# First mixer: convolution sums in PSUM, unscaled turning of the scores with a late division, bias tables loaded, the scan's small matrices spread

## The chip, the cores and the metric

The kernel runs on one core of one Trainium2 chip. The metric is device time in microseconds. Engines by the names of the profile: PE (matmul; PEld loads its stationary operand), DVE (VectorE), ACT (ScalarE), POOL (GpSimd), SP (which issues most DMAs). [...]

## The reference, cut to what matters

A two-layer encoder over 512 tokens of width 1024. Layer 0 has the mixer of this case:

```python
def conformer_conv(a_val, a_gate, conv_w, conv_b, ln_g, ln_b):
    h = a_val * sigmoid(a_gate)
    h = depthwise_conv(h, conv_w, width 31, centred) + conv_b   # 512 channels
    return silu(layernorm(h, ln_g, ln_b))

def even_mixer(h, w_in, ...):
    a_val, a_gate, q, k, v = split(h @ w_in)
    conv_out = conformer_conv(a_val, a_gate, ...)
    # 8 heads of 64; q, k rms-normed per head
    # three dilated windows, each softmax(q k^T / 8 - slope_h * dist), joined by
    # the softmax of their log-sum-exps
    return concat(conv_out, att) @ w_out
```

The three windows are one softmax over all 512 keys with the bias `log(count of windows that hold the pair) - slope_h * dist`, and that is how the kernel computes them. After the mixer comes a routed mixture of 16 experts, in layer 1 an S5 scan (whose discretised matrices are computed from the parameters `lam_re, lam_im, log_dt`) and a second mixture.

## The kernel before, in words

The program is written in the order in which each engine is to run it: no scheduler moves instructions, each engine takes its own in program order, and semaphores stand where data pass between engines. `mixer0` (L310) has these stretches:

- **Input, 0 to 32 us.** Norm and transposition of x, split into a high and a low part (`xT`), so that a product of three fp32r matmuls per 128 rows (`mm3`, L276) replaces one fp32 matmul. Weights come in blocks of 128 by 2048 (1 MB) over the SP queue into a ring of two buffers; `next_split` (L259) turns a block into `whi` (ACT, L273) and `wlo` (L274, on POOL, or on DVE with `fast`). A block's ring buffer is given back, and the next load issued, once it is split. The split blocks lie alternately in the pools `ipa` and `ipb`, one buffer each.
- **Value and gate, 32 to 66 us.** Four chunks of 128 channels, each a pair of products of 24 matmuls; then sigmoid (ACT) and the product with the value (`hp`, L405, DVE), which frees the two `mm` banks. Chunk by chunk the convolution is queued as a generator of 31 DVE instructions (`conv`, L332: one `tensor_scalar`, L334, then 30 `scalar_tensor_tensor`, L337, which add to `cv` in SBUF). `fill.run(ns)` (L49) issues such instructions until their nominal lengths (400, 663) fill `ns`; the list `FL` says how many go where.
- **q, k, v, to 169 us.** Six blocks (n = 0 to 5) of four tiles of 24 matmuls, 128 by 256. `head_norm` of a tile (square on ACT, L554 sum on DVE, root, L559, L562) comes one tile late, with fill around it; `head_turn` (eight transposes, L192) after the second tile of the next block.
- **Attention, 169 to 273 us.** Seventeen steps; step n handles a pair of heads j = n // 4 and a quarter t of the queries: `recip(n)` (1/sum, and two diagonal matrices `dg`, L465), `scores(n+1)`, `soft(n+1)` (add bias and take the maximum, L451; exp with its sum, L456), `values(n-1)`, `turn(n)`: matmuls with `dg` that transpose the exponentials and divide them at once (L474), copied to SBUF by ACT. `bias` (L429) builds a 128x896 table per head on DVE (L432) from `dist` and `logc`. Three convolution instructions are filled in per step; from step `L0` = 6 one step of the convolution's layer norm follows each; silu at step 14, `ln_out` at 15. At `W0` = 11 and 12 half a block of `w_out` is split, on DVE. `s5_small` (L1003) computes the scan's small matrices in 281 instructions, nearly all on POOL and 128x64; it is started once the q, k, v stretch has been issued and yields twice, before the copies of its table `L` to `PV` and `PC` by ACT and DVE (at steps 7 and 8).
- **Output product, 273 to 335 us.** `w_out` in four blocks, 16 products, with the router's work between; the ring of expert weights opens at its start (`rings`, L632).

Of the kernel before, what the change touches and what calls it, by code (L numbers as in the profile page):

```python
# [20 lines left out]
NT = 4  # L21
# [17 lines left out]
S5N = 7  # L39
L0 = 6  # L40
W0 = 11
WM = 36, 55, 14, 5
FL = 8500, 600, 700, 1700, 1000, 1900


class Fill:
# [13 lines left out]
    def drain(self):  # L60
        self.run(1 << 40)

# [44 lines left out]
class Kern:  # L107
# [202 lines left out]
    def mixer0(self, prep, front):  # L310
# [4 lines left out]
        with ExitStack() as c:  # L315
# [16 lines left out]
            def conv(ch):  # L332
                acc = cv[:, ch]
                v.tensor_scalar(acc, hp[:, ch, 0:S], cw[:, ch, 0:1], cb[:, ch:ch + 1], op0=OP.mult, op1=OP.add)  # L334
                yield 400
                for j in range(1, CW):
                    v.scalar_tensor_tensor(acc, hp[:, ch, j:j + S], cw[:, ch, j:j + 1], acc, op0=OP.mult, op1=OP.add)  # L337
                    yield 663

            with ExitStack() as c2:  # L340
# [69 lines left out]
                self.late_consts()  # L410
                if prep:
                    self.s5_params(mp)

# [3 lines left out]
                dist = mp2.tile([128, 896], F32, name="dist")  # L417
                nc.scalar.dma_start(dist, a["dist"])
                logc = mp2.tile([128, 896], F32, name="logc")
                nc.scalar.dma_start(logc, a["logc"])  # L420
# [22 lines left out]
                def soft(n):  # L443
                    j, t = n // 4, n % 4
                    z = un[n]
                    z["sc"], z["dg"] = [], []
                    u = 384 - 128 * t
                    st = mp2.tile([128, 2, 4], F32, name="ast", bufs=4)
# [8 lines left out]
                    z["st"] = st  # L457

                def recip(n):
                    z = un[n]  # L460
                    st = z["st"]
                    v.reciprocal(st[:, :, 3], st[:, :, 2])
                    for i in range(2):
# [110 lines left out]
                for n in range(6):  # L574
# [3 lines left out]
                    for t in range(NT):  # L578
# [7 lines left out]
                        if n == 5 and t == 0:  # L586
                            bias(0)
# [18 lines left out]
            for n in range(N + 1):  # L606
                if n < N:
                    recip(n)
# [1246 lines left out]
```

## Time and profile before

| | |
|---|---|
| median of 3 runs | 1597.78 us (1596.94 to 1600.73) |
| profiled execution | 1601.47 us, its span 1599.7 us |
| PE busy | 1437.1 us (90%) |
| DVE busy | 760.9 us (48%) |
| ACT busy | 368.7 us (23%) |
| POOL busy | 487.2 us (30%) |
| convolution, L337 | 120 instructions, 121.4 us, mean 1012 ns |
| mixer 0 | about the first 335 us of the span |

How to read it: a busy share is an average over stretches with different limits. "Idle before" of a group is time in which its engine stood still ahead of the group, with the instruction that ended it. [...] L-numbers are lines of the kernel before.

### The profile page before, as it was taken

How to read it: one execution, taken by the hardware profiler on the slowest of the kernel's cores; microseconds unless marked ns; L12 is line 12 of the kernel's file. 1: busy time of each engine (PE TensorE's matmuls, PEld its weight loads, DVE VectorE, ACT ScalarE, POOL GpSimd, SP SyncE). 2: the span in 40 equal slices, each digit the busy share in tenths (PEclk: the TensorE clock that was granted, in tenths of full speed). 3: DMA queues.
4: the chain of work that ended last, by engine and by line, in shares of the span. 5: the costliest groups of instructions: out<-in, count | busy, mean ns of one | idle time of the engine just before them, and what ended most of it. 6: DMA issues, size and time to landing. Idle time of an engine off the chain costs nothing. (4 is left out here: it accounts for less than half of the span.)

```text
span 1599.7 us, 23281 instructions
## 1 busy us (share of the span) xinstructions
PE 1437.1 (90%) x9452; PEld 864.2 (54%) x9452; DVE 760.9 (48%) x1200; ACT 368.7 (23%) x776; POOL 487.2 (30%) x749
## 2 busy tenths in 40 slices
PE   8879888989999999897989775899899999999998
PEld 7778656983443443433344664898533333333335
DVE  4999847350238557575612699423311222221122
ACT  5223446320111111111111521336211111111111
POOL 3425887000025576665510456430100000000000
PEclk9989979989999999999999977999999999999999
DMA  4311004539988999999999985822399999999998
GB/s 160 136 53 54 1 1 158 212 132 360 410 349 340 416 416 412 411 409 416 416 418 419 294 267 177 342 106 106 150 420 419 420 419 419 420 419 420 420 419 330
DMA packets 77708, 482.45 MB, mean 302 GB/s; under 512 B 10017, under 2 KB 12833, under 8 KB 23713
## 3 DMA queue, kind: packets, MB, share of 16 engines
q1 hardware_dynamic: 66032, 455.11, 71.0%
q0 software_dynamic: 5504, 16.19, 2.7%
q10 hardware_dynamic: 6064, 9.66, 1.7%
q8 instruction: 74, 1.21, 0.3%
q14 instruction: 34, 0.27, 0.0%
HBM read 456.88 MB, written 24.05 MB: 301 GB/s over the span
## 5 line engine op out<-in xcount | busy, mean ns | idle before, releaser
L825 PE MATMUL mm<-w,xi 128*64 128x512 f32 x2048 | 472.8, 605 | 39.8 <-DMA w<-in_w_e_up 31.7
L825 PEld LDWEIGHTS mm<-w,xi 128*64 128x64 f32 x2048 | 139.3, 138 | 325.3 <-issue 245.8
L877 PE MATMUL po<-w,h 128*64 128x512 f32 x896 | 205.5, 599 | 0.0
L337 DVE SCALAR_TENSOR_TENSOR cv<-hp,vec,cv 128x512 f32<-128x512 f32 x120 | 121.4, 1012 | 2.9
L877 PEld LDWEIGHTS po<-w,h 128*64 128x64 f32 x896 | 59.0, 136 | 106.2 <-issue 104.5
L767 DVE TENSOR_TENSOR R<-R,ac 128x512 f32<-128x512 f32 x112 | 71.8, 682 | 91.9 <-PE ac L765 91.9
L284 PE MATMUL mm<-whi,xT 128*128 128x256 f32 x512 | 101.4, 297 | 11.9 <-DVE hp L405 10.8
L274 POOL TENSOR_TENSOR wlo<-w,whi 128x1024 fp32r<-128x1024 f32 x26 | 67.1, 2603 | 120.3 <-ACT whi L273 120.3
L850 DVE TENSOR_TENSOR h<-h,mm 128x256 f32<-128x256 f32 x60 | 22.5, 417 | 158.1 <-PE mm L825 158.1
L284 PEld LDWEIGHTS mm<-whi,xT 128*128 128x128 f32 x512 | 85.5, 203 | 14.3 <-DVE hp L405 7.3
L284 PE MATMUL mm<-wlo,xT 128*128 128x256 f32 x256 | 75.2, 294 | 0.0
L849 ACT ACTIVATE h<-mm 128x256 f32<-128x256 f32 x60 | 19.8, 381 | 221.3 <-PE mm L825 221.3
L198 DVE COPY OE<-po 64x512 f32<-64x512 f32 x28 | 19.4, 694 | 105.1 <-ACT OE L196 105.0
L694 DVE TENSOR_TENSOR xi<-tr,vec 128x512 f32<-128x512 f32 x32 | 22.1, 691 | 98.2 <-PE tr L704 57.5
L1578 POOL DMA_DIRECT2D gn<-in_mix_norm_odd x8 | 4.7, 592 | 194.0 <-PE mm L825 156.3
L704 PEld LDWEIGHTS tr<-Dm,hn 128*128 128x128 f32 x512 | 59.4, 196 | 7.3 <-ACT h L849 6.5
L1293 PE MATMUL ac<-w,Hs 128*64 128x128 f32 x256 | 33.9, 402 | 31.7 <-POOL Hs L1280 26.5
L196 ACT ACTIVATE OE<-po 64x512 f32<-64x512 f32 x28 | 16.5, 590 | 194.4 <-PE po L877 194.4
L704 PE MATMUL tr<-Dm,hn 128*128 128x128 f32 x512 | 60.9, 281 | 0.0
L284 PEld LDWEIGHTS mm<-wlo,xT 128*128 128x128 f32 x256 | 52.1, 204 | 0.0
L689 DVE TENSOR_TENSOR Dm<-slot,io 128x512 f32<-128x512 f32 (+1 forms) x16 | 11.4, 711 | 85.2 <-PE tr L192 85.1
L1695 POOL DMA_DIRECT2D Ld<-Lt x32 | 18.4, 581 | 108.6 <-DVE Lt L986 102.4
(395 smaller groups left out, 2550.3 us busy)
## 6 DMA issues: line engine op xcount, KB each, us to landing
w<-in_w_e_gate SPq DMA_DIRECT2D x128, 1024.0 KB, 17.0
w<-in_w_e_up SPq DMA_DIRECT2D x128, 1024.0 KB, 17.1
w<-in_w_e_down SPq DMA_DIRECT2D x112, 1024.0 KB, 16.0
w<-in_w_e_tail SPq DMA_DIRECT2D x16, 1024.0 KB, 19.9
w<-in_w_in SPq DMA_DIRECT2D x9, 1024.0 KB, 4.8
Wd<-Wt ACTq DMA_DIRECT2D x32, 256.0 KB, 10.3
Cd<-CE POOLq DMA_DIRECT2D x16, 512.0 KB, 13.0
w<-Wd SPq DMA_DIRECT2D x8, 1024.0 KB, 14.6
```

Of the source, the lines that this page charges most:

```text
L198: self.nc.vector.tensor_copy(out, in_)
L274: (nc.vector if fast else nc.gpsimd).tensor_tensor(lo[:, o], w[:, o], hi[:, o].bitcast(F32), op=OP.subtract)
L284: self.nc.tensor.matmul(out, st(i, k), mv(j, k), start=n == 0, stop=n == 3 * KC - 1)
L337: v.scalar_tensor_tensor(acc, hp[:, ch, j:j + S], cw[:, ch, j:j + 1], acc, op0=OP.mult, op1=OP.add)
L694: v.tensor_tensor(P[j]["xi"][:, 4 * hf:4 * hf + 4], p.rearrange("p (k c) -> p k c", k=4), g[:, 4 * hf:4 * hf + 4].unsqueeze(2).to_broadcas ...
L704: nc.tensor.matmul(p[:, k * 128:(k + 1) * 128], hn[:, s, kk * 128:(kk + 1) * 128], Dm[:, s].rearrange("p e c -> p (e c)"), start=s == 0, s ...
L767: v.tensor_tensor(rv, rv, p, op=OP.add)
L825: nc.tensor.matmul(p[hf * 64:(hf + 1) * 64], xi[:, k, r:r + CAP], w[:, o:o + 512], start=k == 0, stop=k == KC - 1)
L849: nc.scalar.activation(h[:, o], pg[:, o], AF.Silu)
L850: v.tensor_tensor(h[:, o], h[:, o], pu[:, o], op=OP.mult)
L877: nc.tensor.matmul(po[dh * 64:(dh + 1) * 64], hT[:, c4 * 128 + hf * 64:c4 * 128 + hf * 64 + 64], w[:, o:o + 512], start=i == 0, stop=i == 7)
L1293: nc.tensor.matmul(ov, lh, rh, start=n == 0, stop=n == 2)
```

## The change

1. **Convolution.** `conv` takes a PSUM bank (`self.ac()`) as its accumulator; 29 of the 30 adding instructions read and write it, and the last writes the result to `cv` in SBUF.
2. **Turning.** `turn` transposes the unscaled exponentials (PE transposes against the identity); the copies to SBUF go to ACT for the first head and DVE for the second. `recip` comes after `turn` and makes `dg` on ACT. After the fourth quarter of a head pair, `values` spreads the reciprocals over 64 rows with eight fp32 matmuls (`ones` against `dg`) into an `ac` bank, ACT copies them (`zs`), DVE multiplies (`o`), and only then come the high part (ACT) and the low part (DVE).
3. **Softmax.** The negation of the maximum and the exponential are issued head by head.
4. **Bias.** Eight finished tables come from memory over the SP queue (0.46 MB each): two before q, k, v, four after them, two at step 8. The tables' pool and that of `dg`, `zs`, `o` lie on the right side of SBUF, opened after `iq` and `ipb` are closed.
5. **Scan matrices.** `s5_small` returns a list of 281 single instructions; six are issued per tile of q, k, v (24 tiles), 14 per attention step, so that the list ends at step 9. The temporaries of its exponential get buffers of their own.
6. **Order.** The layer norm starts at step 3 (silu at 11, `ln_out` at 12 and 13); `w_out`'s first block is split at 10 and 11; all splits of `w_out` go to POOL instead of DVE.
7. **Fill.** `FL` goes from 8500, 600, 700, 1700, 1000, 1900 to 9200, 600, 1300, 2000, 1300, 1900. By the nominal lengths that is 14 instead of 13 per chunk, 3 per q and k tile as before, 4 instead of 3 per tile of the first v block, 2 per tile of the second as before.

```diff
-S5N = 7
-L0 = 6
-W0 = 11
+L0 = 3
+W0 = 10
+SM = 6, 14
-FL = 8500, 600, 700, 1700, 1000, 1900
+FL = 9200, 600, 1300, 2000, 1300, 1900
...
             def conv(ch):
-                acc = cv[:, ch]
+                acc = self.ac()
...
-                    v.scalar_tensor_tensor(acc, hp[:, ch, j:j + S], cw[:, ch, j:j + 1], acc, op0=OP.mult, op1=OP.add)
+                    v.scalar_tensor_tensor(cv[:, ch] if j == CW - 1 else acc, hp[:, ch, j:j + S], cw[:, ch, j:j + 1],
+                                           acc, op0=OP.mult, op1=OP.add)
...
-                def bias(j):
-                    for h in (2 * j, 2 * j + 1):
-                        B = Bh[h] = mp2.tile([128, 896], F32, name="B", bufs=2)
-                        v.scalar_tensor_tensor(B, dist, -(2.0 ** (-(h + 1))), logc, op0=OP.mult, op1=OP.add)
+                def bias(h, pool, bufs):
+                    Bh[h] = pool.tile([128, 896], F32, name="B", bufs=bufs)
+                    nc.sync.dma_start(Bh[h], a["bias"][h])
...
+                        v.tensor_scalar(st[:, i, 1:2], st[:, i, 0:1], -1.0, None, op0=OP.mult)
                         z["sc"].append(sc)
-                    v.tensor_scalar(st[:, :, 1], st[:, :, 0], -1.0, None, op0=OP.mult)
-                    for i in range(2):
-                        nc.scalar.activation(z["sc"][i], z["sc"][i], AF.Exp, bias=st[:, i, 1:2], accum_out=st[:, i, 2:3])
+                        nc.scalar.activation(sc, sc, AF.Exp, bias=st[:, i, 1:2], accum_out=st[:, i, 2:3])
...
                         for kc in range(4):
-                            nc.tensor.matmul(p[:, kc * 128:(kc + 1) * 128], z["sc"][i][:, kc * 128:(kc + 1) * 128],
-                                             z["dg"][i], start=True, stop=True)
-                        self.copy(z["pt"][:, i].rearrange("p k q -> p (k q)"), p, "v" if n == N - 1 else "a")
+                            self.transpose(p[:, kc * 128:(kc + 1) * 128], z["sc"][i][:, kc * 128:(kc + 1) * 128])
+                        self.copy(z["pt"][:, i].rearrange("p k q -> p (k q)"), p, "av"[i])
+
+                def recip(n):
+                    st, dg = un[n]["st"], []
+                    v.reciprocal(st[:, :, 3], st[:, :, 2])
+                    for i in range(2):
+                        dg.append(late["p"].tile([128, 128], F32, name="dg", bufs=10))
+                        nc.scalar.activation(dg[i], self.ident, AF.Copy, scale=st[:, i, 3:4])
+                    un[n]["dg"] = dg
...
                     if t == 3:
-                        nc.scalar.activation(at[0][:, j], self.pv, AF.Copy)
-                        v.tensor_tensor(at[1][:, j], self.pv, at[0][:, j].bitcast(F32), op=OP.subtract)
+                        p = self.ac()
+                        for tt in range(NT):
+                            for i in range(2):
+                                nc.tensor.matmul(p[i * 64:i * 64 + 64, tt * 128:(tt + 1) * 128], ones[:, :64],
+                                                 un[4 * j + tt]["dg"][i], start=True, stop=True)
+                        zs = late["p"].tile([128, S], F32, name="zs")
+                        nc.scalar.activation(zs, p, AF.Copy, scale=512.0)
+                        o = late["p"].tile([128, S], F32, name="o")
+                        v.tensor_tensor(o, self.pv, zs, op=OP.mult)
+                        nc.scalar.activation(at[0][:, j], o, AF.Copy)
+                        v.tensor_tensor(at[1][:, j], o, at[0][:, j].bitcast(F32), op=OP.subtract)
...
-                if n in (S5N, S5N + 1) and prep:
-                    next(small)
+                little(SM[1])
                 if n in (W0, W0 + 1):
-                    half = self.next_split(ipa, 1, True, n - W0)
+                    half = self.next_split(ipa, 1, False, n - W0)
```

## Rows read from the trace of the kernel before

**Rows 1.** Page of the profile, part 2, 40 slices of 40 us: share of DMA.

```profile
DMA  4311004539988999999999985822399999999998
```

**Rows 2.** Busy time by stretch (columns: stretch, length, engines, PEclk, DMA, GB/s).

```profile
32.00:66.50 34.50, 34.35 (x149) 27.48 (x147) 32.12 (x26) 9.08 (x11) 19.68 (x10) 1.00 0.37 128
66.50:85.70 19.20, 8.48 (x49) 8.25 (x48) 18.67 (x21) 3.67 (x4) 5.16 (x2) 0.74 0.31 107
85.70:168.85 83.15, 73.51 (x565) 71.46 (x565) 80.11 (x126) 26.59 (x59) 40.79 (x39) 0.94 0.14 51
168.85:273.40 104.55, 84.91 (x621) 62.36 (x620) 68.64 (x172) 53.80 (x111) 90.93 (x238) 0.89 0.10 35
273.40:335.00 61.60, 58.50 (x485) 57.21 (x485) 23.77 (x55) 23.53 (x56) 0.82 (x2) 0.97 0.52 211
300.00:330.00 30.00, 29.39 (x254) 29.22 (x254) 9.39 (x23) 8.82 (x24) 0.00 (x0) 1.00 0.10 36
```

**Rows 3.** Who waited for whom, 32 to 169 us: total, times, longest.

```profile
PE mm L284 <- DVE hp L405: 10.8, 2, 7.1
PE tr L192 <- DVE bt L562: 8.8, 4, 2.9
```

**Rows 4.** Timeline of DVE: start, length, line, shapes, count.

```profile
69.90 7.28 DVE L337 SCALAR_TENSOR_TENSOR cv<-hp,vec,cv 128x512 f32<-128x512 f32 x4
...
88.49 1.53 DVE L337 SCALAR_TENSOR_TENSOR cv<-hp,vec,cv 128x512 f32<-128x512 f32 x2
```

**Rows 5.** Timeline of all engines, 17 to 19 us.

```profile
17.68 2.38 POOL L274 TENSOR_TENSOR wlo<-w,whi 128x1024 fp32r<-128x1024 f32 x1 [2.42 <-ACT whi L273]
18.22 0.75 DVE L374 SCALAR_TENSOR_TENSOR xT<-tr,vec,xT 128x512 fp32r<-128x512 f32 x1 [0.77 <-ACT xT L373]
```

**Rows 6.** Timeline of POOL.

```profile
69.89 5.16 POOL L274 TENSOR_TENSOR wlo<-w,whi 128x1024 fp32r<-128x1024 f32 x2 [8.17 <-ACT whi L273]
...
156.45 0.78 POOL L980 TENSOR_TENSOR t<-t,xr 128x64 f32<-128x64 f32 x1
...
196.68 0.32 POOL L980 TENSOR_TENSOR t<-t,t 128x64 f32<-128x64 f32 x1
197.09 0.37 POOL L990 TENSOR_SCALAR t<-t 128x64 f32<-128x64 f32 x1
```

**Rows 7.** The chain that ended last, later places with the same operations.

```profile
1088.68 2.87 PE mm L284 x24
...
1148.11 0.60 PE tr L192 x4
```

**Rows 8.** Who waited for whom, 168.85 to 280 us.

```profile
PE tr L474 <- DVE dg L465: 13.2, 6, 7.3
DVE PV L198 <- POOL L L983: 6.2, 1, 6.2
```

**Rows 9.** Groups by line and shape, 168.85 to 273.4 us: busy us, mean ns.

```profile
L474 PE MATMUL tr<-dg,bt 128*128 128x128 f32 x256 | 37.5, 306 | 13.5 <-DVE dg L465 13.2 <-PE mm L439 0.2
L465 DVE TENSOR_SCALAR dg<-ident,ast 128x128 f32<-128x128 f32 x32 | 10.0, 354 | 0.7
L432 DVE SCALAR_TENSOR_TENSOR B<-dist,logc 128x896 f32<-128x896 f32 x6 | 6.6, 1142 | 0.0
L274 DVE TENSOR_TENSOR wlo<-w,whi 128x1024 fp32r<-128x1024 f32 x2 | 3.6, 1778 | 1.3 <-ACT whi L273 1.3
L491 DVE TENSOR_TENSOR xT<-po,xT 128x512 fp32r<-128x512 f32 x3 | 2.1, 692 | 6.2 <-ACT xT L490 6.2
L490 ACT ACTIVATE xT<-po 128x512 fp32r<-128x512 f32 x3 | 1.7, 573 | 0.0
L526 PE MATMUL ac<-dg,ones 128*128 128x128 f32 x8 | 1.6, 300 | 0.8 <-DVE dg L525 0.7
L517 ACT ACT_TABLE_LOAD x1 | 1.3, 1283 | 0.0
```

**Rows 10.** Timeline of ACT at the end of the attention loop.

```profile
269.82 5.01 ACT L534 ACTIVATE hp<-cv,vec 128x512 f32<-128x512 f32 x4
```

More of the change, by code (lines that the diff above doesn't have):

```diff
@@ L410, in mixer0, with little @@
                 self.late_consts()
+                small = []
                 if prep:
                     self.s5_params(mp)
+                    small = self.s5_small(c_mix.enter_context(self.pool("sq")))
+                def little(n):
+                    while n and small:
+                        small.pop(0)()
+                        n -= 1
                 at = [t[:, 0:4] for t in xT]
@@ L427, in mixer0 @@
                 Bh = {}
-                def bias(j):
-                    for h in (2 * j, 2 * j + 1):
-                        B = Bh[h] = mp2.tile([128, 896], F32, name="B", bufs=2)
-                        v.scalar_tensor_tensor(B, dist, -(2.0 ** (-(h + 1))), logc, op0=OP.mult, op1=OP.add)
+                def bias(h, pool, bufs):
+                    Bh[h] = pool.tile([128, 896], F32, name="B", bufs=bufs)
+                    nc.sync.dma_start(Bh[h], a["bias"][h])
+                for h in range(2):
+                    bias(h, mp2, 2)
+                late = {}
                 def scores(n):
@@ L585, in mixer0 @@
                             turned = None
-                        if n == 5 and t == 0:
-                            bias(0)
+                        little(SM[0])
                         if n == 5 and t == 1:
@@ L599, in mixer0 @@
                     w = wn
-            if prep:
-                small = self.s5_small(c_mix.enter_context(self.pool("sq")))
-                next(small)
+            late["p"] = c_mix.enter_context(self.pool("attn2", side="right"))
+            for h in range(2, 6):
+                bias(h, late["p"], 4)
             wo = []
             for n in range(N + 1):
-                if n < N:
-                    recip(n)
                 if n + 1 < N:
@@ L615, in mixer0 @@
                     turn(n)
-                if n + 2 < N and (n + 2) % 4 == 0:
-                    bias((n + 2) // 4)
+                    recip(n)
+                if n == 8:
+                    bias(6, late["p"], 4)
+                    bias(7, late["p"], 4)
                 fill.run(FL[5])
@@ L620, in mixer0 @@
                     steps[n]()
-                if n in (S5N, S5N + 1) and prep:
-                    next(small)
+                little(SM[1])
                 if n in (W0, W0 + 1):
-                    half = self.next_split(ipa, 1, True, n - W0)
+                    half = self.next_split(ipa, 1, False, n - W0)
+            little(-1)
             wo.append(half)
@@ L1003, in s5_small, with copy @@
     def s5_small(self, q):
-        nc, tc, a = self.nc, self.tc, self.a
-        v = nc.gpsimd
+        out = []
+        v, dve = Later(self.nc.gpsimd, out), Later(self.nc.vector, out)
         mul, sub, add, ts, fma = self.arith(v)
+        def copy(o, x, eng):
+            out.append(lambda: self.copy(o, x, eng))
         PV, PC, PP, F, dg, rho = self.PV, self.PC, self.PP, self.F, self.dg, self.rho
@@ L1018, in fexp @@
         def fexp(x):
[L1019 to L1020 removed]
+            n, t, r, e = tl(), tl(), tl(), tl()
+            i = q.tile([128, G], I32, name=f"xi{cnt[0]}")
             ts(n, x, 1.4426950408889634, -126.0, OP.mult, OP.max)
@@ L1151, in s5_small @@
             unit(PP, j)
-        yield
+        return out
     def s5_phase(self, o, sp, br):
@@ L1730, in build @@
                 k.s5_params(q)
-                list(k.s5_small(q))
+                for f in k.s5_small(q):
+                    f()
         if f0:
@@ L1835, in prep @@
     m = (d <= 64).astype(int) + ((d % 4 == 0) & (d <= 256)) + (d % 16 == 0)
-    a["dist"] = d.astype(f)
-    a["logc"] = np.where(m > 0, np.log(np.maximum(m, 1)), NEG).astype(f)
+    logc = np.where(m > 0, np.log(np.maximum(m, 1)), NEG).astype(f)
+    a["bias"] = np.stack([logc - d.astype(f) * f(2.0 ** -(h + 1)) for h in range(H)])
     return a
```

48 lines of the change are left out of this document (18 added, 30 removed).

## The prediction

> **What bounds the kernel now.** First I read the slices of the page: from slice 9 (360 us) DMA is 90% busy or nearly so for some 500 us [rows 1]. There the first mixture streams its weights, and the change has no hand in it. I then asked whether a shorter mixer moves that stream. Between 300 and 330 us DMA is busy only 0.10 [rows 2]: the expert ring has been filled and waits for buffers, which come free when PE begins the experts. So the stream starts by the end of mixer and router, and what is saved before 335 us comes off the total one for one. Then I took the mixer in stretches [rows 2]:
>
> - 32 to 66.5: PE 34.35 of 34.5 busy. PE is the bound.
> - 66.5 to 168.85 (two rows, 102.35 us): DVE 98.8 busy, PE 82.0, part of that at a clock of 0.74 and 0.94. DVE is the bound; PE waits 10.8 us for `hp` and 8.8 for normed heads, which stand behind the convolution on DVE [rows 3].
> - 168.85 to 273.4: nobody is full (PE 85 of 104.6, POOL 91, DVE 69, ACT 54). A chain through three in-order engines is the bound.
> - 273.4 to 335: PE 58.5 of 61.6.
>
> Last I asked why a convolution instruction takes a mean of over 1 us. Two of them take 1.53 alone, starts 0.72 apart; four take 7.28 when POOL's split runs from 69.89 to 75.05 [rows 4, 6]. An instruction that reads two SBUF operands stands still while POOL works, and POOL suffers likewise: a small product takes 0.78 beside the convolution, 0.32 without it [rows 6].
>
> **The change, part by part.** The sum is made on the profiled execution (1601.47 us, span 1599.7), 3.7 above the median of the runs; the difference is carried over.
>
> *Convolution in PSUM.* No row shows DVE writing PSUM or adding to it. The nearest is L374: the same operation with one operand in PSUM, 0.75 while POOL's split ran over it, and that split took 2.38, not the 2.6 to 2.8 beside the convolution [rows 5]. So I take 0.72 from start to start and no more standing still. Bounds: 0.72 (alone) and 1.8 (7.28 for four, as if nothing had been gained).
>
> [...]
>
> *66.5 to 168.85.* With 0.72 the 14 fills and `hp` of a chunk (1.1) take 11.2 us, PE's 48 matmuls 11.3, so `hp` of the last chunk is done at about 68, and PE, which has a third bank, doesn't wait. A q or k tile costs DVE three fills (2.16) and 0.82 of norm: 2.98, so 11.9 a block. PE needs four tiles of 2.87 and eight transposes at 0.9 (two rows of 0.60, overlapped): 12.4 [rows 7]. So PE becomes the bound: 11.5 for n = 0, four times 12.4, 12.6 for n = 5 with a pair of scores: 73.7 us.
>
> What is late next is POOL. It gets 24 small instructions per block ahead of the next split. Free they start 0.41 (product) and 0.45 (scalar) apart, mean 0.42; a split of two halves is 4.8 [rows 5, 6]: 14.9 a block against PE's 12.4. POOL has a lead: the split for n = 1 ends at about 73.6 (now it starts at 69.89; ACT has two DMA issues less ahead of it), that for n = 2 at 86.2 (needed at 90.4), for n = 3 at 101.2 (102.8), for n = 4 at 116.2 (115.2), for n = 5 at 131.2 (128.6). PE waits 1.0 and 2.6: 3.6 us. The stretch takes 77.3, ends at 143.8 and saves 25.0. The first `FL` entries only move convolution forward; ten instructions are left for attention.
>
> *Attention, saved.* DVE's 6.6 for bias tables and 3.6 for two half splits go, both in the chain, since the next scores wait behind them [rows 9]. The longest wait, 7.3 of PE for `dg`, was DVE standing 6.2 for POOL's table `L` [rows 8]. Now the copies come at step 0; POOL has `L` ready at about 149.4 (131.2 and 43 more, the last ones a little cheaper: 18.2), DVE reaches the copies at 143.8 + 5.4, so this wait is gone, without margin. Five convolution instructions fewer: 3.6. Together 21.
>
> *Attention, added.* Z: eight fp32 matmuls, at 0.25 each (four show as eight records, 1.6 busy with overlap) 2.0; then `zs` 0.57, `o` 0.69 and 0.4, an estimate, for hand-overs: 3.7 more from the last `values` to `at` [rows 9]. Behind it stand on ACT and DVE the copies of the next `pt`, so three boundaries cost 11. Silu's 5.0 stood after the last exponential; at step 11 it blocks ACT, with its own table load and one to bring exp back (1.28 each), for 7.6, of which the other engines cover about 1.5: 6 [rows 9, 10]. Together 17.
>
> *Attention, even.* The transposes take PE from 2.0 to about 0.95 a step, but PE isn't the bound. DVE loses two `dg` (10.0 in all) and gains one copy of 0.69 in 16 steps; ACT the reverse [rows 9]. Negating head by head adds 0.2 on DVE and starts exp earlier. Net of the stretch: 4 saved, and I keep 12 saved to 6 lost, as the terms overlap in ways that a sum can't show.
>
> *The rest.* Bias loads are 3.7 MB where DMA is busy 0.10 to 0.14 [rows 2]. The first two pass SP between blocks, some 80 us early; the next four wait on SP for `ipb` and are needed 15 us later; the last two sit ahead of `w_out`'s third block, which waits for a split anyway. The splits on POOL take 4.8 instead of 2.4 for a block, and each has an earlier product to hide in (11.5 us; the last only 5.8, where at most 0.5 shows). The expert ring reuses the memory of `dg` and `o`, so it starts at the end of attention as now; 30 us of slack cover it. The last `at` comes 3.7 later, but seven eighths of the first product (2.5) go ahead of it: 1 lost.
>
> **Sum.** 25.0 + 4 - 1 = 28 saved: 1601.5 - 28 = 1573.5 for a profiled run, 1570 for the median.
>
> **Rivals.**
>
> *POOL sets the pace (the other side).* Place: the splits behind the small instructions. Price p per instruction; the split for n = 5 ends at 73.6 + 20p + 72p + 19.2, block 5 takes 12.6 more, and step 0's copies then wait for 48p - 18. The saving vanishes when 105.4 + 92p + (48p - 18) reaches 168.85 + 3, so at p = 0.60. At 0.87, today's price beside the convolution (0.78 and a gap) [rows 6], the stretch ends at 185.4 and 23.8 of waiting follow: 37 slower, 1635. For it: 0.87 is what most of the first small instructions pay now. Against: its cause is the operand pair that the change removes, and at 196.68, beside instructions with one PSUM operand, the price is 0.32 [rows 6]. At p = 0.50 the stretch ends at 151.4 and 6 of waiting follow: 1584.
>
> *Adding in PSUM is dear.* Place: DVE in the q, k tiles. A tile is 0.82 + 3c. Today a block is four tiles of 2.98 and the two halves of a split, which hold four instructions for 7.28 - 2.88 = 4.4 longer [rows 4]: 16.3, or 4.08 a tile, which c = 1.09 gives too. Above that the kernel is slower: at 1.3 the 114 instructions ahead of attention cost 0.29 more than today's mean of 1.01, 33 us: 1631. For it: no row of such an instruction. Against: L374.
>
> *The clock falls in attention.* PE's work there falls from 85 to about 70 us in as long a stretch, and gaps go with a granted clock of 0.74 in 66.5 to 85.7 and 0.89 in attention [rows 2]. At 0.75 PE's 70 would grow by some 12, a part of it in the chain: 8, 1578. Gaps may also let the boundary chains cost twice my 11: 1581.
>
> *The saving is absorbed*, the mixture not following the mixer: 1598. For it: DMA-bound from 360 us [rows 1]. Against: the 30 us with a full ring.
>
> **How the numbers follow.** Forecast, 1560 to 1581: 0.60. Attention shorter than reckoned (7.3-type waits gone, boundaries hidden), 1550 to 1560: 0.08. Clock or boundaries, 1578 to 1592: 0.13. POOL at 0.5 or more: 0.10, half of it below 1593. PSUM dear: 0.06. Absorbed: 0.03. Faster by over 0.3% (below 1593; 0.3% is about what a measurement of this kernel can tell from no change) is 0.60 + 0.08 + 0.13 + 0.05 = 0.86; within 0.3%: absorbed and 0.01 of POOL, 0.04; slower: 0.04 of POOL and 0.06, 0.10. The range 1554 to 1592 leaves out the slow cases and a part of the fast one.
>
> **What would show it.** Right: L337 near 0.75 with no member above 1; PE without waits for `hp`; q, k, v ending near 144; the granted clock 1.00 until then; POOL's small instructions 0.32 to 0.38; PE's short waits for `wlo` from n = 4 on; attention still about 100 us, with `at` late at each boundary and ACT closed at step 11. Wrong: a mean of L337 over 1, waits of PE for `wlo` of over 5 us, DVE waiting for `L` at step 0, or the mixture's stream starting where it starts now.

## The result, and the profile after

| | time, us | profiled execution, span |
|---|---|---|
| before | 1597.36 median (1595.65 to 1600.73, 4 runs) | 1601.47, 1599.7 |
| after | 1573.38 median (1571.09 to 1576.14, 4 runs) | 1575.44, 1573.4 |

The ratio is 0.9848, 95% interval 0.9822 to 0.9874: 24 us saved, where 1570.0 (1554 to 1592) was forecast. The direction and the size were right. Below it turns out that the parts were not: one of the edits by itself earns more than the whole, and at least three of the others cost time as they stand.

Three places in the traces mark off the parts: the second pair's scores (the end of q, k, v), DVE's low part of the last piece of `at` (the end of attention), and DVE's first multiplication in the first expert. Before (columns: start, length, engine, line, operation, tiles, shapes, count, idle time before it and what ended it):

```profile
168.85 1.13 PE L439 MATMUL mm<-qT 64*128 64x512 f32 x4
...
276.82 0.68 DVE L491 TENSOR_TENSOR xT<-po,xT 128x512 fp32r<-128x512 f32 x1
...
377.65 0.75 DVE L850 TENSOR_TENSOR h<-h,mm 128x256 f32<-128x256 f32 x2 [7.26 <-PE mm L825]
```

and after:

```profile
146.38 1.13 PE L458 MATMUL mm<-qT 64*128 64x512 f32 x4
...
247.40 0.69 DVE L517 TENSOR_TENSOR xT<-o,xT 128x512 fp32r<-128x512 f32 x1 [0.70 <-ACT xT L516]
...
348.71 0.75 DVE L876 TENSOR_TENSOR h<-h,mm 128x256 f32<-128x256 f32 x2 [7.26 <-PE mm L851]
```

The scores of the second pair start at 146.38 instead of 168.85. So q, k, v saved 22.5 us, attention 6.9 (107.97 long before, 101.02 after), and the output product lost 0.5 (100.83 to 101.31): 28.9 at the first expert. At the end of the span 26.3 is left (1599.7 to 1573.4); the other 2.6 are lost inside the first mixture, where DMA's mean busy share is 1.0 (490 to 820 us).

Busy time by stretch after, in answer to [rows 2] (the last row is attention):

```profile
66.50:85.70 19.20, 15.97 (x119) 15.59 (x117) 18.71 (x32) 6.60 (x11) 11.69 (x23) 0.91 0.31 105
85.70:110.00 24.30, 24.30 (x208) 24.30 (x207) 23.53 (x49) 10.15 (x25) 21.33 (x41) 1.00 0.26 88
110.00:145.00 35.00, 34.19 (x282) 33.02 (x281) 32.99 (x59) 13.20 (x29) 30.72 (x73) 1.00 0.17 61
146.40:247.40 101.00, 75.09 (x574) 51.22 (x574) 57.86 (x161) 63.72 (x137) 51.75 (x143) 0.85 0.12 41
```

From 85.7 us to attention PE is busy almost without a gap at a granted clock of 1.00, the full one, where it was the engine that waited. In attention PE has fewer microseconds of work and a lower clock than before (0.85 against 0.89 in [rows 2]).

The group of the convolution (count, busy us, mean ns); `ac` is one of two PSUM tiles of 128x512 fp32 values, beside which the program has three `mm`, two `tr` and one `po`:

```profile
L348 DVE SCALAR_TENSOR_TENSOR ac<-hp,vec,ac 128x512 f32<-128x512 f32 x116 | 87.3, 752 | 3.0
```

DVE's timeline around the last chunk of value and gate, in answer to [rows 4]:

```profile
66.03 5.51 DVE L348 SCALAR_TENSOR_TENSOR ac<-hp,vec,ac 128x512 f32<-128x512 f32 x7
71.45 1.07 DVE L417 TENSOR_TENSOR hp<-mm,sg 128x512 f32<-128x512 f32 x1
72.37 3.02 DVE L71 TENSOR_TENSOR t<-lam 128x64 f32<-128x64 f32 x2
...
75.56 1.54 DVE L348 SCALAR_TENSOR_TENSOR ac<-hp,vec,ac 128x512 f32<-128x512 f32 x2
```

No convolution instruction stands still any more: 752 ns in the mean where it was 1012. But two instructions that weren't in the forecast do: `den` and `d1`, small products of the S5 matrices with two SBUF operands, now queued here, take 0.66 and 2.44 us. Each ends as the half split that POOL is at does (73.02 and 75.38, the halves at 72.95 and 75.30). POOL, in answer to [rows 6]:

```profile
70.54 4.77 POOL L284 TENSOR_TENSOR wlo<-w,whi 128x1024 fp32r<-128x1024 f32 x2 [8.98 <-ACT whi L283]
...
85.12 4.75 POOL L284 TENSOR_TENSOR wlo<-w,whi 128x1024 fp32r<-128x1024 f32 x2 [1.97 <-ACT whi L283]
...
98.89 0.33 POOL L71 TENSOR_TENSOR t<-t,t 128x64 f32<-128x64 f32 x1
99.30 0.37 POOL L71 TENSOR_SCALAR t<-t 128x64 f32<-128x64 f32 x1
```

A half split takes 2.4 and a small instruction 0.32 to 0.38, as forecast. The last split starts at 129.40, 14.6 to 14.9 after the one before it.

PE's waits from 66.5 to 250 us, in answer to [rows 3, 8] (in all, times, longest):

```profile
PE po L502 <- ACT bt L206: 17.1, 8, 8.8
PE ac L552 <- DVE dl L551: 5.8, 1, 5.8
PE mm L294 <- DVE bt L589: 3.1, 1, 3.1
```

The waits for `hp` (0.2 is left), for the normed heads as they were and for `dg` are gone, and so is DVE's for `L`: it copies `PV` at 152.15 without a wait. New are 3.1 for the normed head that stood behind `den` and `d1`, and two long ones in attention: 5.8 for `dl`, which the reciprocal of the layer norm's root makes at step 8, and 8.8 for the copy of a turned score. For the longest, ACT around step 11, in answer to [rows 10]:

```profile
216.27 1.28 ACT L560 ACT_TABLE_LOAD   x1
217.57 4.87 ACT L560 ACTIVATE hp<-cv,vec 128x512 f32<-128x512 f32 x4
222.34 1.04 ACT L283 ACTIVATE whi<-w 128x1024 fp32r<-128x1024 f32 x1
223.40 1.28 ACT L474 ACT_TABLE_LOAD   x1
...
226.12 0.57 ACT L513 ACTIVATE zs<-ac 128x512 f32<-128x512 f32 x1
```

For 8.4 us ACT does none of attention's work; behind it stand the next two exponentials, `zs` of the head pair that ends there, and the copy of a turned score for which PE waits 8.85. In what follows a boundary is such a place, where the fourth quarter of a head pair is done and Z, `zs` and `o` are made.

### The profile page after: what moved, and what is told of

Same layout as the page of the kernel before. It is cut to its first block, busy times and chain, and to the rows that moved or that the text cites. A ratio compares the mean times of both kernels' runs of the same rounds, so it can differ in the third digit from the quotient of the medians.

```text
span 1573.4 us, 23168 instructions
## 1 busy us (share of the span) xinstructions
PE 1415.7 (90%) x9388; PEld 843.2 (54%) x9388; DVE 718.7 (46%) x1186; ACT 376.1 (24%) x799; POOL 476.6 (30%) x757
## 5 line engine op out<-in xcount | busy, mean ns | idle before, releaser
L284 POOL TENSOR_TENSOR wlo<-w,whi 128x1024 fp32r<-128x1024 f32 x30 | 71.4, 2400 | 100.9 <-ACT whi L283 100.9
L294 PE MATMUL mm<-whi,xT 128*128 128x256 f32 x512 | 96.1, 287 | 4.0 <-DVE bt L589 3.1
L348 DVE SCALAR_TENSOR_TENSOR ac<-hp,vec,ac 128x512 f32<-128x512 f32 x116 | 87.3, 752 | 3.0
L294 PEld LDWEIGHTS mm<-whi,xT 128*128 128x128 f32 x512 | 81.3, 193 | 5.5 <-ACT sqh L579 3.2
L790 PE MATMUL ac<-OH,DT 128*128 128x512 f32 x112 | 50.3, 449 | 0.0
## 6 DMA issues: line engine op xcount, KB each, us to landing
w<-in_w_e_gate SPq DMA_DIRECT2D x128, 1024.0 KB, 17.5
Wd<-Wt ACTq DMA_DIRECT2D x32, 256.0 KB, 10.3
```

The costliest lines, as they stand in the source:

```text
L284: (nc.vector if fast else nc.gpsimd).tensor_tensor(lo[:, o], w[:, o], hi[:, o].bitcast(F32), op=OP.subtract)
L294: self.nc.tensor.matmul(out, st(i, k), mv(j, k), start=n == 0, stop=n == 3 * KC - 1)
L348: v.scalar_tensor_tensor(cv[:, ch] if j == CW - 1 else acc, hp[:, ch, j:j + S], cw[:, ch, j:j + 1], acc, op0=OP.mult, op1=OP.add)
L790: nc.tensor.matmul(p, DT, P[j]["hi"], start=True, stop=False)
```

## The experiments

Times in us. "Scores", "at" and "h" are the starts of the first scores on PE, of DVE's low part of the last `at`, and of DVE's first expert multiplication, in each kernel's profiled execution; the last columns are all runs. The runs of one kernel lie 2.6 to 8.2 apart. Kernels with the same program up to the first scores (after, SiLU at the end, scaled turning, norm two steps later) reach them at 137.6 to 138.8, so a difference of 1 us in a place says nothing. The kernels ran in five series, in which the kernel before took 1597.4 to 1598.9 in the median; each ratio is to its own series.

| kernel | scores | at | scores to at | h | median | ratio to before, 95% |
|---|---|---|---|---|---|---|
| before | 161.1 | 276.8 | 115.8 | 377.7 | 1597.4 | |
| after | 138.6 | 247.4 | 108.8 | 348.7 | 1573.4 | 0.9848 (0.9822 to 0.9874) |
| convolution alone | 133.4 | 237.5 | 104.1 | 338.4 | 1563.8 | 0.9782 (0.9754 to 0.9811) |
| all but the convolution | 174.6 | 282.1 | 107.5 | 383.6 | 1608.5 | 1.0060 (1.0036 to 1.0083) |
| SiLU at the end | 138.8 | 241.5 | 102.7 | 341.9 | 1566.8 | 0.9808 (0.9781 to 0.9835) |
| ten per tile | 163.3 | 267.7 | 104.4 | 367.6 | 1593.7 | 0.9975 (0.9964 to 0.9987) |
| small matrices in blocks | 133.7 | 240.5 | 106.8 | 340.4 | 1567.3 | 0.9798 (0.9773 to 0.9822) |
| den on POOL | 136.6 | 244.4 | 107.8 | 344.3 | 1568.8 | 0.9812 (0.9793 to 0.9831) |
| scaled turning | 138.1 | 240.6 | 102.5 | 343.0 | 1565.0 | 0.9789 (0.9774 to 0.9805) |
| norm two steps later | 137.6 | 235.0 | 97.4 | 336.3 | 1562.5 | 0.9770 (0.9749 to 0.9791) |
| tables built | 138.4 | 249.5 | 111.0 | 349.3 | 1575.9 | 0.9854 (0.9835 to 0.9874) |
| combined | 134.5 | 228.1 | 93.6 | 328.5 | 1554.4 | 0.9720 (0.9704 to 0.9735) |
| combined, last step on DVE | 133.6 | 225.5 | 91.9 | 326.4 | 1550.7 | 0.9702 (0.9689 to 0.9715) |
| combined, scaled turning | 134.5 | 223.4 | 88.9 | 324.3 | 1546.7 | 0.9678 (0.9654 to 0.9702) |

**The convolution alone.** The kernel before, with:

```diff
-                acc = cv[:, ch]
+                acc = self.ac()
...
-                    v.scalar_tensor_tensor(acc, hp[:, ch, j:j + S], cw[:, ch, j:j + 1], acc, op0=OP.mult, op1=OP.add)
+                    v.scalar_tensor_tensor(cv[:, ch] if j == CW - 1 else acc, hp[:, ch, j:j + S], cw[:, ch, j:j + 1],
+                                           acc, op0=OP.mult, op1=OP.add)
```

> The kernel before, with one edit: the convolution's running sum is held in PSUM, and its last member writes the SBUF buffer. Theory A (the operand pair, and not the rest of the change, carries the q, k, v stretch): the convolution's mean falls from 1012 ns to about 755; POOL has no small instructions between its splits here, so PE finds every split in time, and the stretch from 66.5 us, 102.35 us before, takes about 75 to 80 and ends at 142 to 147. Attention keeps its 104.6 us, with the waits for dg and for L in it. First multiplication of the first expert's result on DVE: 377.65 - 24 = 353 to 355; total 1597.4 - 24 = 1573, about the same as the whole change. Theory B (the early small matrices, the two DMA issues and the bias tables matter too): the stretch ends at 155 or later, and the total stays above 1582.

Measured: 1563.8, the first multiplication at 338.4, 10.3 earlier than with the whole change. Theory A holds for q, k, v, but the total is 9 below it, as attention didn't keep its length: it is 11.7 shorter, and the one edit in it is that of the 21 convolution instructions that are filled in there. Their own length hardly changes (0.757 to 0.753 us in the mean). POOL's splits in this kernel:

```profile
69.55 4.77 POOL L274 TENSOR_TENSOR wlo<-w,whi 128x1024 fp32r<-128x1024 f32 x2 [7.72 <-ACT whi L273]
79.68 4.76 POOL L274 TENSOR_TENSOR wlo<-w,whi 128x1024 fp32r<-128x1024 f32 x2 [5.35 <-ACT whi L273]
91.94 4.78 POOL L274 TENSOR_TENSOR wlo<-w,whi 128x1024 fp32r<-128x1024 f32 x2 [7.50 <-ACT whi L273]
```

One of PE's waits from 66.5 to 250 us:

```profile
PE tr L475 <- DVE dg L466: 6.2, 5, 1.6
```

POOL idles ahead of every split, so nobody waits for `wlo`. PE's wait for `dg` falls from 13.2 [rows 8] to 6.2, because DVE no longer waits for `L`: POOL's small instructions start at 121.3 and mostly start 0.41 to 0.46 apart instead of 0.87, so `L` is there when step 7 asks for it. The other 4.7 of the 11.7 aren't separated; the clock of attention is 0.96 here.

**All but the convolution.** The changed kernel with `acc = cv[:, ch]`.

> The changed kernel, with one edit undone: the convolution adds up in SBUF as before. Theory A (DVE and POOL slow each other whenever DVE's instruction has two SBUF operands, and everything else in the change lives from that going): the convolution's mean is 1000 ns or more; POOL's small product beside it takes 0.78 and not 0.32, so its 24 per block take some 21 us and the splits stand behind them; the stretch ends at about 185, where the copies of L wait again, and the total comes to about 1635, slower than the kernel before. Rival (only the convolution's own time counts): the stretch ends where DVE brings it, at about 169, attention keeps its saving of 6, and the total is about 1591.

Measured: 1608.5, slower than before, between theory A's 1635 and the rival's 1591; the convolution's mean is 0.95 us. POOL between two splits:

```profile
104.04 0.72 POOL L71 TENSOR_SCALAR t<-t 128x64 f32<-128x64 f32 x1
...
119.55 0.73 POOL L71 TENSOR_TENSOR t<-t,t 128x64 f32<-128x64 f32 x1
```

DVE at the first split, which lasts from 70.44 to 75.74, and behind it:

```profile
71.56 4.72 DVE L348 SCALAR_TENSOR_TENSOR cv<-hp,vec,cv 128x512 f32<-128x512 f32 x2
76.21 0.54 DVE L345 TENSOR_SCALAR cv<-hp,vec 128x512 f32<-128x512 f32 x1
76.78 4.69 DVE L348 SCALAR_TENSOR_TENSOR cv<-hp,vec,cv 128x512 f32<-128x512 f32 x6
```

Theory A's mechanism is there, both ways: a split stops DVE (two instructions in 4.72), DVE's pairs double the time of POOL's small instructions (0.72 and 0.73 here, 0.37 and 0.33 in the changed kernel). Its price was too high: the 24 between the splits at 97.25 and 120.25 took 17.5, so 0.73 each and not 0.87, and DVE ran a convolution instruction for 12.6 of the 17.5. The scores start at 174.6, 36 later than after, and attention's saving isn't eaten by `L` (DVE waits 0.8 for it), so the 23.8 of waiting at step 0 that made 1635 didn't come.

**SiLU at the end.** The changed kernel with:

```diff
-                         L0 + 7: lambda: ln_scale((2, 3)), L0 + 8: ln_silu, L0 + 9: lambda: ln_out((0, 1)),
-                         L0 + 10: lambda: ln_out((2, 3))}
+                         L0 + 7: lambda: ln_scale((2, 3)), 14: ln_silu, 15: lambda: ln_out((0, 1, 2, 3))}
```

> The changed kernel, with one edit undone: the SiLU of the four pieces stands at step 14 and the division of the last norm at step 15, as before, instead of at steps 11 to 13. Theory A (the 8.85 us that PE waits at step 11 for the transposed scores are ACT's 7.4 us of SiLU and two table loads): that wait falls to under 2, one table load less; at the end ACT has 6 us in front of the last copies, which cost 3 to 6 there. Attention, 98.8 us, becomes 2 to 5 shorter, and the first multiplication of the first expert's result comes at 344 to 347 instead of 348.71; total 1569 to 1572. Rival (step 11 is covered by what the other engines have still to do): attention no shorter or up to 5 longer, total 1573 to 1579.

Measured: 6.2 off attention, 6.6 off the total. Theory A, and more than it said: at the end the SiLU costs less (PE waits 5.2 for the last copy, where it waited 8.85); no exponential is behind it there.

**Ten small instructions per tile.** The changed kernel with `SM = 10, 14` for `SM = 6, 14`.

> The changed kernel, with one number changed: ten small instructions of the S5 matrices follow each q or k tile on POOL, not six. Theory A (POOL and PE go just in step in q, k, v, and POOL's pace is splits of 4.75 plus 0.42 per small instruction): a block takes 40 x 0.42 + 4.75 = 21.5 us, the split for n = 5 ends at 75.3 + 153 x 0.42 + 4 x 4.75 = 158.4 instead of 134.2, q, k, v end at about 171 instead of 146.4, PE waits some 24 us for wlo, and the total is about 1598, all of the change's gain. Rival (POOL has slack, or the small instructions start no later than their operands allow): under 8 us longer, total below 1582.

Measured: the scores 24.7 later and the total 20.3, near theory A, but only half for its reason. The waits from 66.5 to 180 us:

```profile
ACT PV L206 <- POOL L L71: 16.9, 1, 16.9
DVE PV L208 <- POOL L L71: 16.0, 1, 16.0
PE mm L294 <- DVE bt L589: 13.0, 2, 9.6
...
PE mm L294 <- POOL wlo L284: 10.2, 2, 5.1
```

The first three splits start 19.5 and 21.3 apart, as a pace of 0.42 asks. But with ten per tile the copies of `L` come into DVE's and ACT's queues in the middle of q, k, v, ahead of the head norms, and wait there for POOL. The kernel shows that POOL has no room left; it doesn't measure the pace alone.

**The small matrices in blocks.** The changed kernel with the following; the call `little(145)` stands ahead of the loop over n:

```diff
-SM = 6, 14
+SM = 0, 0
...
+            little(145)
...
-                little(SM[1])
+                little({7: 6, 8: -1}.get(n, 0))
```

> The changed kernel, with one edit undone: the small S5 instructions are not spread over q, k, v and attention; 145 go to the queues ahead of attention and the rest at steps 7 and 8, as before. With the convolution alone changed the first scores stood at 133.4 us, in the changed kernel at 138.6. Theory A (spreading is what costs those 5.2: DVE's two products of the block stand behind POOL's split, and POOL's splits come later): the first scores come at 133 to 134, POOL waits between its splits as in that run, attention keeps its length or loses up to 1, and the first multiplication of the first expert's result on DVE comes at 343 to 345 instead of 348.71; total 1568. Rival (the 5.2 come from the bias tables' loads or the first FL entries): first scores stay at 138 to 139, total 1573 or more, as POOL's block then also holds up its splits at steps 10 and 11.

Measured: scores at 133.65, total 1567.3. Theory A, with the first multiplication at 340.4 even earlier than its 343: spreading cost 4.9 in q, k, v and 2.0 in attention. The tables' loads and the `FL` entries are cleared.

**den on POOL.** The changed kernel with:

```diff
-        for o, x, y, op in ((den, lr, lr, OP.mult), (d1, li, li, OP.mult), (den, den, d1, OP.add)):
-            dve.tensor_tensor(o, x, y, op=op)
-        dve.reciprocal(den, den)
+        mul(den, lr, lr)
+        mul(d1, li, li)
+        add(den, den, d1)
...
         mag = fexp(x)
+        dve.reciprocal(den, den)
```

> The changed kernel, with the two products and the sum of den on POOL instead of DVE, and the reciprocal, still on DVE, some 40 small instructions later. Theory A (DVE's stand of 3.0 us behind POOL's split is the start of the loss): DVE's stand and the 3.1 us that PE waits for the normed head go, the granted clock of 66.5 to 85.7 is 1.00 instead of 0.91, and POOL has no idle before its second split; but POOL's pace of 14.8 a block then decides, the last split ends at about 134.15 - 1.97 + 1.2 = 133.4, so PE waits 2 to 3 us for wlo and the first scores come only 1 earlier, at 137.5 to 138; total about 1572. Rival (POOL is early enough, PE alone decides): first scores at 134.5 to 135.5, total 1569 to 1570.

Measured: the scores at 136.56, between the two theories, the total, 1568.8, just below the rival's 1569. DVE's stand and PE's 3.1 for the head are gone, and POOL goes on without idle, so that its pace shows:

```profile
69.79 4.77 POOL L284 TENSOR_TENSOR wlo<-w,whi 128x1024 fp32r<-128x1024 f32 x2 [9.10 <-ACT whi L283]
...
83.84 4.75 POOL L284 TENSOR_TENSOR wlo<-w,whi 128x1024 fp32r<-128x1024 f32 x2
```

One of PE's waits from 66.5 to 180 us:

```profile
PE mm L294 <- POOL wlo L284: 2.2, 3, 1.2
```

The stand was worth 2.0 of the 5 that spreading costs; of the rest 2.2 is POOL's pace, PE's wait for `wlo`.

**Scaled turning.** The changed kernel with `turn`, `recip` and the end of `values` as before (matmuls with `dg`, `dg` on DVE, no Z, `zs` and `o`; the last step's copies on DVE).

> The changed kernel, with one edit undone: the scores are turned by multiplication with dg, which scales them, and the values are not divided afterwards (no Z, zs and o); dg is made on DVE again. Theory A (turning unscaled gives and takes about the same, as the PE's work in attention isn't the bound): DVE's waits for zs, 17.8, go, PE waits for dg instead; from the first scores to the last piece of at, 108.8 us, it takes 105 to 112, total 1570 to 1577. Rival (the chain reciprocal, dg, product stands in every step's path, and taking it out is where attention got shorter): 115 or longer, total above 1579.

Measured: 102.5 from scores to `at`, total 1565.0, below both theories: where the norm and the SiLU stand in the changed kernel, the new turning and division cost 6.3. PE's waits:

```profile
PE po L503 <- DVE xT L509: 6.9, 1, 6.9
PE tr L482 <- DVE dg L492: 3.0, 3, 1.8
PE ac L544 <- DVE dl L543: 2.7, 1, 2.7
```

The chain that the change was to shorten is worth 3.0 here. Where the norm's root meets a boundary (steps 7 and 8), the values of neighbouring steps start 8.0 apart, against 12.8 after; where the SiLU does, 11.0 against 12.9.

**The norm two steps later.** The changed kernel with `L0 = 5` for `L0 = 3`.

> The changed kernel, with one number changed: the last norm's work starts at step 5 instead of 3 (L0 = 5), so its root with two table loads falls on step 9, away from the boundary of a group of heads, and the SiLU on step 13. In the changed kernel the values of two neighbouring steps start 12.8 us apart where root and boundary meet, and 12.9 apart where SiLU and boundary meet; elsewhere 4 to 7. Theory A (ACT's blocks cost much only where they stand ahead of zs at a boundary): both gaps shrink, the first to 8, the second to 9 to 11; from the first scores to the last piece of at 98 to 102 instead of 108.8, total 1563 to 1568. Rival (the blocks cost the same wherever they stand): 106 or more, total 1571 or above.

Measured: 97.4 from scores to `at`, total 1562.5: one number is worth 11 us, a little more than theory A said. But theory A's reason holds in part only. The gap between the values at the root's old boundary shrinks from 12.8 to 8.0, that at the SiLU's from 12.9 to 5.7. The SiLU, two steps off the boundary, opens a new gap of 10.1: the next exponentials and copies stand behind it there too. PE's wait behind the SiLU in the changed kernel:

```profile
228.62 0.69 PE L502 MATMUL po<-bt,vt 128*64 128x128 f32 x2 [8.85 <-ACT bt L206]
```

and in this one:

```profile
225.97 1.98 PE L502 MATMUL po<-bt,vt 128*64 128x128 f32 x16 [7.98 <-ACT bt L206]
```

From the first scores to the values of step 11, which in both kernels come ahead of the SiLU, 10.0 of the 11.4 are gained (77.2 to 67.2), and only 1.4 behind them. So for the SiLU the rival is nearer, and the gain is that of the rest of the norm. All its parts moved with the number, so they aren't separated; PE's wait for `dl` falls from 5.8 to 1.4.

**The tables built on DVE.** The changed kernel with:

```diff
-                def bias(h, pool, bufs):
-                    Bh[h] = pool.tile([128, 896], F32, name="B", bufs=bufs)
-                    nc.sync.dma_start(Bh[h], a["bias"][h])
+                def bias(j):
+                    for h in (2 * j, 2 * j + 1):
+                        B = Bh[h] = mp2.tile([128, 896], F32, name="B", bufs=2)
+                        v.scalar_tensor_tensor(B, dist, -(2.0 ** (-(h + 1))), logc, op0=OP.mult, op1=OP.add)
```

and the two loads of `dist` and `logc`, and the calls where they were.

> The changed kernel, with one edit undone: the bias tables are built on DVE from two loaded tables, two heads at a time, instead of being loaded. Theory A (6.6 us of DVE stand in the chain of attention, two of the eight tables ahead of it): attention or the stretch before it 5 to 7 longer, the first multiplication of the first expert's result at 354 to 356, total 1579 to 1580. Rival (DVE has room: it waits 17.8 for zs and 13.8 for scores): 0 to 2 longer, total 1573 to 1576.

Measured: attention 2.2 longer, but the first multiplication only 0.6 later; total 1575.9, 2.5 longer with overlapping intervals. The rival: most of DVE's 6.6 of tables fall where it waits anyway.

**Combined.** The changed kernel with den on POOL, `SM = 5, 14`, `L0 = 5`, SiLU at 14 and the division of the norm at 15.

> The changed kernel, with four edits: den on POOL as in the other run, five small instructions per tile instead of six, the SiLU back at step 14 and the division at step 15, and the last norm's work two steps later (L0 = 5), so that its root isn't at the boundary of a group of heads. From the runs so far: the first scores come at 133.5 to 134.5 (138.6 in the changed kernel, 133.4 with the convolution alone), since POOL's four blocks get 16 instructions less (6.7 us); from there to the last piece of at 100 to 103 instead of 108.8 (102.7 with the SiLU at the end; the norm's root and dl cost another 0 to 3). First multiplication of the first expert's result at 335 to 339; total 1559 to 1564, as fast as or up to 5 faster than the convolution alone (1563.8). If the parts overlap instead of adding, it stays at 1566 to 1570.

Measured: 1554.4, better than expected: attention takes 93.6.

**Combined, with scaled turning.** The same, with turning and division as before.

> The combined kernel (den on POOL, five per tile, SiLU at 14, L0 = 5; 93.7 us from the first scores to the last piece of at, 1554.4 in all), but with the scores turned by multiplication with dg, made on DVE, and no division afterwards. Theory A (the division costs only where ACT's blocks stand ahead of zs; without them turning unscaled saves dg's place in every step's chain): 95 to 100, total 1556 to 1561. Rival (turning unscaled loses by itself, 6.3 us in the changed kernel): 87 to 90, total 1548 to 1551.

Measured: 88.9 and 1546.7, the fastest of all: 27 us below the changed kernel. The numbers are the rival's, not theory A's. Busy time of attention in the combined kernel:

```profile
146.00:229.00 83.00, 66.19 (x560) 46.48 (x561) 55.85 (x158) 60.62 (x134) 51.67 (x142) 0.94 0.14 45
```

and in this one:

```profile
146.00:222.00 76.00, 74.15 (x614) 54.83 (x613) 52.01 (x164) 54.97 (x110) 51.88 (x143) 1.00 0.19 66
```

With scaled turning PE has 8 us more to do and is busy 74 of 76 at full clock; without, ACT has 5.6 more, and PE waits 14.6 for ACT's copies. Until step 12 the values start at the same times within 1.4 (206.84 and 206.55 for that step). The loss is at the end. ACT of the combined kernel there:

```profile
215.57 1.28 ACT L560 ACT_TABLE_LOAD   x1
216.87 4.91 ACT L560 ACTIVATE hp<-cv,vec 128x512 f32<-128x512 f32 x4
221.68 0.57 ACT L206 ACTIVATE bt<-tr 128x512 f32<-128x512 f32 x1
```

and its PE:

```profile
222.31 1.97 PE L502 MATMUL po<-bt,vt 128*64 128x128 f32 x16 [5.38 <-ACT bt L206]
224.06 1.92 PE L510 MATMUL ac<-dg,ones 128*64 128x128 f32 x16
225.92 0.58 PE L294 MATMUL mm<-whi,xT 128*128 128x256 f32 x1
```

The last copy and the last `dg` stand behind the SiLU. With scaled turning both are on DVE, and the product starts on PE at 220.26.

**Combined, the last step on DVE.** The combined kernel with:

```diff
-                        self.copy(z["pt"][:, i].rearrange("p k q -> p (k q)"), p, "av"[i])
+                        self.copy(z["pt"][:, i].rearrange("p k q -> p (k q)"), p, "v" if n == N - 1 else "av"[i])
...
-                        nc.scalar.activation(dg[i], self.ident, AF.Copy, scale=st[:, i, 3:4])
+                        if n == N - 1:
+                            v.tensor_scalar(dg[i], self.ident, st[:, i, 3:4], None, op0=OP.mult)
+                        else:
+                            nc.scalar.activation(dg[i], self.ident, AF.Copy, scale=st[:, i, 3:4])
```

> The combined kernel (1554.4 us, first multiplication of the first expert's result at 328.48), with one more edit: in the last step both copies of the turned scores and the two dg go to DVE, so that nothing of the last values and of Z is queued on ACT behind the SiLU. With the scores turned scaled (1546.7, 324.31) the values start at the same times up to step 12, and the output product starts on PE at 220.3 instead of 225.9; in the combined kernel PE waits 5.4 us for the last copy, which stands behind SiLU's 4.91 and its table load. Theory A (turning unscaled loses through what it queues on ACT, here at the end alone): the last values start at 218 to 219 instead of 222.3, the output product at 221 to 222, the first multiplication at 324.5 to 326, total 1549 to 1551. Theory B (the division loses by itself, through Z, zs, o and their hand-overs): values as early, but the product still at 224 or later, and the total at 1553 or more.

Measured: the last values at 218.63 and the product early:

```profile
218.63 0.43 PE L505 MATMUL po<-bt,vt 128*64 128x128 f32 x2 [0.41 <-DVE bt L208]
...
221.12 0.39 PE L294 MATMUL mm<-whi,xT 128*128 128x256 f32 x1
```

Total 1550.7, as theory A has it; the first multiplication comes at 326.4, a little late for it. From the values of step 13 to that multiplication it takes 113.6, like the 113.2 with scaled turning, against 116.6. So the end is settled: ACT's queue, not the division. Of the 4.2 between the two combined kernels, though, this kernel gets back 2.0 only. From its first scores to the values of step 13 it takes 79.3, and the others 77.5 and 76.6. But up to that step its program is that of the combined kernel, so 79.3 against 77.5 is how far two executions of one program lie apart here, and whether scaled turning gains anything ahead of the end isn't shown. The intervals of this ratio and of that with scaled turning overlap.

## Why the prediction was right

Its total is right, its map of the gain only in part.

- **The mixer's time comes off the total.** Right: the 28.9 still stand, within 1 us, at 490 us. The 2.6 lost afterwards, between 493 and 820 us, where DMA's mean busy share is 1.0, were not forecast and not studied.
- **Convolution in PSUM.** No standing still, as L374 had let expect [rows 5]; the price was mis-sized, through a misread row. A run of dependent members takes 0.785 each (7 in 5.51), not 0.72. The two members of [rows 4] don't start 0.72 apart but 0.78; another instruction, L554 at 89.93, follows the second one after 0.66, and 0.72 is the mean of the two. With sums in SBUF and no split beside it, it is 0.78 as well (4.69 for six, in the kernel without the convolution's edit). What follows the pair of [rows 4] in the kernel before:

```profile
89.93 0.41 DVE L554 TENSOR_REDUCE st<-sqh 128x4 f32<-128x256 f32 x1
```

- **q, k, v.** Forecast 77.3 us and 25.0 saved; measured 79.9 and 22.5. PE became the bound and the clock 1.00, as said. The step that failed is the list of what is queued where: the early small instructions were counted on POOL alone, but two of the first are DVE's and have two SBUF operands. They took 3.0 beside POOL's split, and the head norm stood behind them. The pace of POOL, 14.9 a block, was right to 0.3. PE's waits for `wlo`, forecast 3.6, were 0.2, since PE was itself late; with den on POOL they are 2.2.
- **What the early start of the small matrices brings.** Counted as a gain (the 7.3 of `dg`, the 6.2 of `L` [rows 8]). Both waits go with the convolution alone (of `dg`'s the longest left is 1.6), since POOL then works at its own price. Spreading is a loss of 4.9 ahead of the scores and 2.0 behind them.
- **Bias tables.** 6.6 in the chain [rows 9]: mis-sized. In the changed kernel it is 0.6 at the first multiplication, and 2.5 in the total with overlapping intervals; in the kernel before it wasn't tried. The row shows busy time of an engine that waited elsewhere in the same steps.
- **SiLU at step 11.** 6 lost: right, 6.2 gained by undoing it. But it isn't the boundary that makes it dear. From the values of step 11 to `at` it takes 31.7 with the SiLU at step 11, 30.3 at step 13, off the boundary, and 27.1 at the end.
- **Division.** 11 lost at the boundaries, the transposes even: 6.3 net in the changed kernel. Right in sign and in naming `zs` and the copies of the next `pt`. At the end of attention it is ACT's queue that makes it cost, not the division. The 0.4 for hand-overs was an estimate that no row shows; at the last boundary `zs`, `o`, the high part and the low part each start 0.03 to 0.04 after the end of what they wait for. What was missed is where the norm stands: with its root on the boundary of steps 7 and 8, moving it by two steps gives 10.0 ahead of the SiLU.
- **Attention in all.** 4 forecast, 6.9 measured, with the clock at 0.85 and so lower than before, as that rival had it. The convolution's part was larger than reckoned: from the second pair's scores on 15 of its instructions became 7, eight fewer and not five. What the clock costs wasn't separated from the gaps that go with it.
- **The rivals.** POOL's pace decides on the other side only if the operand pair stays: then the scores come at 174.6. The formula gives 172.8 for the end of the last split, which was at 169.3, but that is luck: with the 0.70 that an instruction took in the mean it gives 157. The rest is 7.8 for which POOL waited ahead of its second split, a first split that ended 2.1 later than reckoned, and splits of 5.3 instead of 4.8. Dear PSUM (over 1.09 each by that rival, 0.785 measured), and a saving absorbed by the mixture, are excluded.

So the sum came out because its errors cancel, which is luck: 4 to 6 too much for the tables, 2.5 too much for q, k, v and nothing charged for where the norm stands, against savings in attention that were reckoned too small. Of those the runs show the convolution's 11.7, and 4.7 of them stay unexplained. The softmax by heads, the splits of `w_out` on POOL and the fill weren't tried by themselves, so the account of attention doesn't close.

## What to carry to other kernels

Try the smallest edit of a bundle by itself first: here it gave 34 us where the bundle gave 24. Of the others some paid once they were moved (1554.4 combined, against 1563.8 for the convolution alone); the turning without scales paid in neither kernel that was compared with and without it. When work is spread over an engine's idle time, list every instruction of it by engine, with its operands' memories and with what is queued behind it. Look for what stands behind a long ACT instruction, wherever it is put: with exponentials and copies behind it, the SiLU (4.87 in the changed kernel, with a table load of 1.28 ahead of it) cost PE 8.85 of waiting at a boundary and 7.98 two steps away; after the last exponential PE waited 5.2 and 5.38, and 0.41 with the last copies on DVE.

## What the runs showed of the hardware

- How long DVE stood still went by POOL's instruction, not by the size of its own. Two 128x64 products with two SBUF operands took 3.02 beside a split, each ending less than 0.1 after a half of it (73.02 and 72.95, 75.38 and 75.30). The same two took 0.48 in the kernel with the convolution alone, where POOL ran small instructions.
- The other way round POOL paid too: its small instructions went from 0.42 to 0.73 apart beside a convolution with sums in SBUF, and a split from 4.77 to between 5.2 and 5.7.
- Gaps on PE and the granted clock went together: in attention the changed kernel, busy 75 of 101 us, was granted 0.85 in the mean, the fastest kernel, busy 74 of 76, 1.00.
